# Gated differential attention: the gates between the two halves of the q, k, v projection, and a reordered prologue

## The chip, the cores and the metric

The kernel runs on one core of one Trainium2 chip. The metric is the device time of one execution in microseconds (us). Beside it stands the span, from the first to the last instruction in the profile of one execution.

## The reference

A residual layer with 1024 tokens of width 1024: row norm, a projection to q, k, v and a gate z (each 2048 wide, 16 heads), differential attention (two score maps for each head, the second subtracted with a weight lambda), a norm for each head, the product with silu(z), and the output projection.

```python
h = rms_norm(x, norm_g)
q, k, v, z = split(h @ w_in, 4)
q = rms_norm(q, q_norm_g) * 64 ** -0.5        # each head: 2 maps of width 64
k = rms_norm(k, k_norm_g)
# causal, with ALiBi bias, for each head and map m
probs = softmax(q_m @ k_m.T - slope * dist)
o = (probs[0] - lam * probs[1]) @ v           # v: 128 wide
o = rms_norm(o, head_norm_g) * (1 - lam0)
return x + (o * silu(z)) @ w_out
```

Products are made in split form: an operand is written as a high part in float16 and a low part (the remainder), and three products (high x high, low x high, high x low) are added in PSUM.

## The kernel before, in words

Everything runs on the core's five engines under a framework that places the instructions of each engine in an order by a simulated timeline; the program's order is a preference, and an instruction moves ahead where its operands are there. Calls inside `pin(...)` (`keep_in_program_order`) keep the program's order among themselves on their engine. Each engine then runs its own list in order.

*Prologue* (lines 217 to 345). For each of eight tiles of 128 tokens, `chain(t)` makes the row norm: a Square on ScalarE (L255), `rsqrt` (VectorE L94, ScalarE's Ln and Exp in L98 and L99, VectorE L100, L101, L103), and the normed tile `htok` by VectorE in L259. TensorE transposes it into PSUM (L275), ScalarE copies the high part `h` out (L277), VectorE makes the low part (L278). The gain `gb` is brought to a power-of-two unit first: its maximum (L240), the unit sg[0] (L241 to L244), and the product with the whole gain (L245). In between stands the split of the first head's weights, `split_w`, a generator that is advanced step by step: eight row maxima (L154), their maximum over the partitions by a product on TensorE (L165, L169), the scales (L172 to L180), the high part on ScalarE (L199), the low part on VectorE (L205, for q and k) or on GpSimd (L202 and L203, for v and the gate: `LO_POOL`).

*Heads.* The loop at line 669 takes the heads in the order 1, 3, ..., 15, 0, 2, ..., 14. In round i, `merge` runs two generators side by side: `attend` of the head before and `project` of this head, at a set ratio (RATE). `project` makes, for two halves c of 512 tokens, four groups of q, k, v (24 matmuls each, L370 to L372) into PSUM tiles `pg`, which ScalarE (L422, L423) and VectorE (L424) copy out, and behind each half `norm(c, rw)` (L376 to L396), which ends in a DMA transpose on SyncE's queue (L393) and two copies (L396). After both halves come the two gates, one for each half (`gate`, L443 to L459): 24 matmuls into a tile `pz` of the same three PSUM banks (`PSG` = 3, tag "pg"), and a chain of six steps over ScalarE and VectorE (L452 to L457) that makes silu; L457 is the last to read the bank. Heads 10, 12 and 14 (`LATE`) make no gate here; theirs come at the end in `late_gates`. Between the groups `prepare` advances the split of the next head's weights: four squares (L160), a step with a small product that needs a free part of a PSUM tile `pb` (and waits where `pb` is None), then L199, L202, L203, L205. In the first head `prepare` is called twice a group, in the others once, and again in the gates.

`attend` makes, for eight steps of 128 queries, the scores on TensorE (L570), a row minimum with the bias on VectorE (L559), the exponentials on ScalarE (L576), the difference and its split (L584, L66, L587) and a DMA transpose on SyncE's queue (L589); the values (L601 to L603) and the head's norm (L609 to L631) follow. Steps 0 to 3 read the first half's q and k, steps 4 to 7 the second's. `finalize` multiplies with the gate.

## Time and profile before

| | us |
|---|---|
| median of 3 runs | 1176.29 |
| lowest and highest | 1174.27, 1181.22 |
| the profiled execution | 1173.53 |
| its span | 1171.8 |
| TensorE busy (share of the span) | 1109.9 (95%) |
| VectorE busy | 883.0 (75%) |
| ScalarE busy | 774.2 (66%) |
| GpSimd busy | 272.2 (23%) |

In the rows, PE is TensorE's matmuls, PEld its weight loads, DVE VectorE, ACT ScalarE, POOL GpSimd, SP SyncE, which issues DMAs; L12 is line 12 of the kernel. A row of the timeline has the start in us, the duration in us, the engine, the line, the operation, output <- inputs, shapes and the count; in brackets stands the idle time of the engine ahead of it and who ended it. Matmuls overlap in the engine, so their durations add up to more than the time.

### The profile page before, as it was taken

The page shows a single profiled execution, that of the slowest core. Times are in us where ns is not written, and L with a number is a line of the kernel's source. Part 1 is how long each engine was busy: PE and PEld are TensorE (multiplying, and loading weights), DVE is VectorE, ACT ScalarE, POOL GpSimd, SP SyncE. Part 2 cuts the span into 40 slices and gives each one's busy share as a digit, 9 for nine tenths or more (in the row PEclk, how much of TensorE's full clock was granted, in tenths as well). Part 3 has the DMA queues.
Part 4 walks back from the last instruction along what each step waited for, and adds up shares of the span by engine and source line. Part 5 has one row for each costly group of instructions (what it writes and reads, how often), then busy time and mean ns, then how long its engine had stood idle before and what let it go on. Part 6 is the DMA issues. An engine that isn't in the chain of part 4 may idle for free.

```text
span 1171.8 us, 18439 instructions
## 1 busy us (share of the span) xinstructions
PE 1109.9 (95%) x6154; PEld 668.5 (57%) x6154; DVE 883.0 (75%) x2180; ACT 774.2 (66%) x1713; POOL 272.2 (23%) x208
## 2 busy tenths in 40 slices
PE   4999999999999999999999999999899997999998
PEld 3555554545555555555545455555455534788887
DVE  6867869787978797879787878788888898563121
ACT  4757778787878797869686978787778776230000
POOL 2220314141314131314131313312121302031000
PEclk7999999999999999999999999999999988999999
DMA  7453736464646464646463645464564457685342
GB/s 222 109 119 52 164 67 140 89 140 85 139 90 137 88 143 89 146 80 133 93 144 76 140 93 126 93 129 100 105 137 87 109 125 182 143 292 179 112 130 70
DMA packets 327887, 143.50 MB, mean 122 GB/s; under 512 B 225136, under 2 KB 307312, under 8 KB 327792
## 3 DMA queue, kind: packets, MB, share of 16 engines
q1 hardware_dynamic: 323040, 133.93, 50.9%
q10 hardware_dynamic: 4752, 8.39, 2.7%
q8 instruction: 48, 0.79, 0.3%
q14 instruction: 47, 0.39, 0.1%
HBM read 63.11 MB, written 16.25 MB: 68 GB/s over the span
## 4 chain that ended last, share of the span: by engine, by line
PE 51%; DVE 20%; ACT 10%; issue 8%; DMA 6%; POOL 2%; SPq 2%; DVEq 0%; ACTq 0%; POOLq 0%
PE pg L370 8%; PE pg L371 8%; PE pg L372 8%; DVE p L559 6%; PE pf L498 5%; PE pf L499 5%; PE pf L500 5%; PE pss L570 3%; DMA raww<-in_l_w_in_dram 3%; DVE p L584 2%; ACT p L576 2%; ACT wsp L160 2%; ACT wsp L199 2%; DMA wt<-p 2%; PE po L601 2%
## 5 line engine op out<-in xcount | busy, mean ns | idle before, releaser
L370 PE MATMUL pg<-wsp,h 128*128 128x384 f16 x1024 | 336.3, 328 | 21.0 <-DVE sz L457 11.9
L372 PE MATMUL pg<-wsp,h 128*128 128x384 f16 x1024 | 336.4, 329 | 1.1 <-DVE h L278 1.1
L371 PE MATMUL pg<-wsp,h 128*128 128x384 f16 x1024 | 336.3, 328 | 1.2 <-POOL wsp L203 1.2
L576 ACT ACTIVATE p<-p,mn 128x128 f32<-128x128 f32 (+7 forms) x256 | 196.4, 768 | 61.0 <-DVE mn L559 59.8
L559 DVE CUSTOM_DVE_ANT_0 p<-pss,toep,nsl 128x512 f32<-128x512 f32 (+3 forms) x256 | 161.2, 642 | 36.8 <-DMA wt<-p 24.6
L570 PE MATMUL pss<-qk 128*128 128x512 f16 (+3 forms) x768 | 164.6, 327 | 11.6 <-DVE mn L559 11.5
L371 PEld LDWEIGHTS <-h 128*128 128x128 f16 x1024 | 100.7, 98 | 86.7 <-issue 26.5
L372 PEld LDWEIGHTS <-h 128*128 128x128 f16 x1024 | 100.6, 98 | 68.2 <-issue 3.7
L66 ACT ACTIVATE p<-p,rc 128x128 f16<-128x128 f32 (+7 forms) x128 | 98.6, 771 | 61.8 <-DVE p L584 60.7
L370 PEld LDWEIGHTS <-h 128*128 128x128 f16 x1024 | 100.7, 98 | 66.6 <-issue 4.1
L584 DVE SCALAR_TENSOR_TENSOR p<-p,rc,p 128x128 f32<-128x128 f32 (+7 forms) x128 | 116.9, 914 | 1.5
L587 DVE SCALAR_TENSOR_TENSOR p<-p,rc,p 128x128 f16<-128x128 f32 (+7 forms) x128 | 104.7, 820 | 14.8 <-ACT p L66 14.6
L570 PEld LDWEIGHTS <-qk 128*128 128x128 f16 x768 | 71.0, 98 | 72.2 <-issue 18.6
L447 PE MATMUL pz<-h,wsp 128*128 128x512 f16 x256 | 98.3, 384 | 1.3 <-DVE sz L457 1.3
L448 PE MATMUL pz<-h,wsp 128*128 128x512 f16 x256 | 98.3, 384 | 0.0
L614 POOL TENSOR_TENSOR sql<-sqo,sqh 128x512 fp32r<-128x512 f32 x30 | 41.7, 1390 | 243.3 <-ACT sqh L612 243.3
L449 PE MATMUL pz<-h,wsp 128*128 128x512 f16 x256 | 98.1, 383 | 0.0
L537 POOL TENSOR_TENSOR sz<-sqo,sz 128x512 f32<-128x512 f32 x26 | 37.7, 1448 | 184.4 <-DVE sqo L631 150.0
L202 POOL TENSOR_SCALAR raww<-raww,scw 128x1024 f32<-128x1024 f32 (+1 forms) x31 | 42.3, 1371 | 159.1 <-ACT wsp L199 127.9
L559 DVE CUSTOM_DVE_ANT_0 p<-pss,toep,mn 128x128 f32<-128x128 f32 (+3 forms) x128 | 75.6, 601 | 0.0
L160 ACT ACTIVATE wsp<-raww 128x1024 f16<-128x1024 f32 x61 | 63.6, 1044 | 14.7 <-DMA raww<-in_l_w_in_dram 9.4
L503 DVE TENSOR_TENSOR xr<-pf,xr 128x512 f32<-128x512 f32 (+1 forms) x33 | 22.1, 671 | 63.4 <-PE pf L500 62.5
(160 smaller groups left out, 2082.9 us busy)
## 6 DMA issues: line engine op xcount, KB each, us to landing
raww<-in_l_w_in_dram SPq DMA_DIRECT2D x96, 256.0 KB, 3.8
rawo<-in_l_w_out_dram SPq DMA_DIRECT2D x32, 256.0 KB, 4.5
qk<-qk SPq DMA_DIRECT2D x64, 128.0 KB, 2.4
raww<-in_l_w_in_dram SPq DMA_DIRECT2D x40, 192.0 KB, 3.7
g_dram<-sz SPq DMA_DIRECT2D x30, 256.0 KB, 2.3
rawg<-g_dram ACTq DMA_DIRECT2D x24, 256.0 KB, 3.5
xt<-in_x_dram SPq DMA_DIRECT2D x8, 512.0 KB, 5.3
xr<-in_x_dram SPq DMA_DIRECT2D x16, 256.0 KB, 3.5
```

Source lines behind the costliest of these rows:

```text
L66: A.activation(out, in_, AF.Copy, scale=scale)
L370: T.matmul(pg, a_h, w_h, start=k == 0, stop=False)
L371: T.matmul(pg, a_h, w_l, start=False, stop=False)
L372: T.matmul(pg, a_l, w_h, start=False, stop=k == KT - 1)
L447: T.matmul(pz, wt["hi"][:, k, n], hh[c][:, k], start=k == 0, stop=False)
L448: T.matmul(pz, wt["hi"][:, k, n], hl[c][:, k], start=False, stop=False)
L449: T.matmul(pz, wt["lo"][:, k, n], hh[c][:, k], start=False, stop=k == KT - 1)
L559: V.tensor_tensor_reduce(out=pm[m][:, o:o + w], in0=pss[:, :w], in1=toep[:, u:u + w], scale=nslope, scalar=3e38 if prev[m] is None else pr ...
L570: T.matmul(pss[m][:, :w].rearrange("p (t q) -> p t q", q=P), qk[:, c, 0, i % 4, m], qk[:, b, v, :w // P, m], start=v == 1, stop=v == 2)
L576: A.activation(pm[m][:, :n], pm[m][:, :n], AF.Exp, scale=-1.0, bias=prev[m], accum_out=sx[:, 1 - m:2 - m])
L584: V.scalar_tensor_tensor(out=p0, in0=p1, scalar=rc[:, 0:1], in1=p0, op0=ALU.mult, op1=ALU.add)
L587: V.scalar_tensor_tensor(out=pl[:, n:], in0=p0, scalar=rc[:, 1:2], in1=pl[:, :n], op0=ALU.mult, op1=ALU.subtract)
```

## The change

Four things. (1) The gain is no longer brought to its unit ahead of the norm: the unit sg[0] is made inside the first `rsqrt` (`gap`) and multiplied in where h is copied out of PSUM, in ScalarE's scale and in a scalar_tensor_tensor on VectorE. (2) The eight row maxima of the first weights, which stood in a block behind the first tile's copies, are called 3, 3 and 2 at a time around them (`bounds`), and the second tile's chain is interleaved with the split. (3) The first head's v block has its high part made by GpSimd instead of ScalarE, and the first product group runs all high x high products, then low x high, then high x low. (4) `project` makes the first half with its norm, then both gates, then the second half with its norm; `prepare` is called twice for each group of the first half and once for each of the second, in every head. The tile `sz` has four buffers instead of three, and `sqo` takes a buffer of the norm's `sqk`.

```diff
--- before.py
+++ after.py
@@ -87,7 +87,7 @@
     eps_t = cp.tile([P, 1], F32, name="eps_t")
     G.memset(eps_t, EPS)
 
-    def rsqrt(sp, src, n, scale, tag, pin=lambda ins: ins, eps=EPS):
+    def rsqrt(sp, src, n, scale, tag, pin=lambda ins: ins, gap=lambda: None, eps=EPS):
 
         v = sp.tile([P, n], F32, name=f"v_{tag}", tag=f"v_{tag}")
         if isinstance(eps, float):
@@ -97,6 +97,7 @@
         y = sp.tile([P, n], F32, name=f"y_{tag}", tag=f"y_{tag}")
         pin(A.activation(y, v, AF.Ln))
         pin(A.activation(y, y, AF.Exp, scale=-0.5))
+        gap()
         pin(V.tensor_tensor(v, v, y, ALU.mult))
         pin(V.scalar_tensor_tensor(out=v, in0=v, scalar=-0.5, in1=y, op0=ALU.mult, op1=ALU.mult))
         r = sp.tile([P, n], F32, name=f"r_{tag}", tag=f"r_{tag}")
@@ -193,8 +194,16 @@
             if not first:
                 rest()
             yield
+            if first:
+                for ks in (slice(0, 4), slice(4, 8)):
+                    src, h_, l_, c_ = raw[:, ks, 2], hi[:, ks, 2], lo[:, ks, 2], sc[:, 2:3]
+                    pin(G.tensor_scalar(h_, src, c_, 1.0, ALU.mult, ALU.mult))
+                for ks in (slice(0, 4), slice(4, 8)):
+                    src, h_, l_, c_ = raw[:, ks, 2], hi[:, ks, 2], lo[:, ks, 2], sc[:, 2:3]
+                    pin(G.tensor_scalar(src, src, c_, 1.0, ALU.mult, ALU.mult))
+                    pin(G.tensor_tensor(l_, src, h_, ALU.subtract))
             for ks in (slice(0, 4), slice(4, 8)) if first else (slice(0, 8),):
-                for j, s_ in enumerate(blocks):
+                for j, s_ in enumerate(blocks[:2] if first else blocks):
                     src, h_, l_, c_ = raw[:, ks, s_], hi[:, ks, s_], lo[:, ks, s_], sc[:, j:j + 1]
                     pin(A.activation(h_, src, AF.Copy, scale=c_))
                     yield
@@ -237,15 +246,17 @@
                     T.transpose(out=tp[:, k], in_=ident, identity=ident)
 
             gt_ = x1.tile([P, 1], F32, name="gt_")
-            V.tensor_reduce(out=gt_, in_=gb, axis=AX.X, op=ALU.max, apply_absolute_value=True)
-            V.tensor_scalar(gt_, gt_, 2.0 ** -20, None, ALU.max)
-            V.tensor_scalar(gt_.bitcast(I32), gt_.bitcast(I32), 0x7F800000, None, ALU.bitwise_and)
-            V.reciprocal(sg[0], gt_)
-            V.tensor_scalar(sg[0], sg[0], 2.0 ** 9, None, ALU.mult)
-            V.tensor_scalar(gb, gb, sg[0], None, ALU.mult)
-            V.tensor_scalar(sg[1], gt_, 2.0 ** -9, None, ALU.mult)
-            V.tensor_tensor(sg[2], sg[0], sg[0], ALU.mult)
-            V.tensor_scalar(sg[2], sg[2], EPS, None, ALU.mult)
+
+            def top_gain():
+                V.tensor_scalar(gt_, gt_, 2.0 ** -20, None, ALU.max)
+                pin(V.tensor_scalar(gt_.bitcast(I32), gt_.bitcast(I32), 0x7F800000, None, ALU.bitwise_and))
+                pin(V.reciprocal(sg[0], gt_))
+                pin(V.tensor_scalar(sg[0], sg[0], 2.0 ** 9, None, ALU.mult))
+
+            def gain_units():
+                V.tensor_scalar(sg[1], gt_, 2.0 ** -9, None, ALU.mult)
+                V.tensor_tensor(sg[2], sg[0], sg[0], ALU.mult)
+                V.tensor_scalar(sg[2], sg[2], EPS, None, ALU.mult)
 
             def chain(t):
                 if t > 0 and len(xts) < NB:
@@ -253,19 +264,30 @@
                 sq = xp.tile([P, D], F32, name="sqx", tag="sqx", bufs=2)
                 ss = xp.tile([P, 1], F32, name="ssx", tag="ssx")
                 pin(A.activation(sq, xts[t], AF.Square, accum_out=ss))
-                r = rsqrt(xp, ss, 1, 1.0 / D, "x", pin)
+                if t == 0:
+                    pin(V.tensor_reduce(out=gt_, in_=gb, axis=AX.X, op=ALU.max, apply_absolute_value=True))
+                yield
+                r = rsqrt(xp, ss, 1, 1.0 / D, "x", pin, gap=top_gain if t == 0 else lambda: None)
                 ht = xp.tile([P, D], F32, name="htok", tag="htok", bufs=3)
                 for cs in (slice(0, 512), slice(512, D)) if t == 0 else (slice(0, D),):
                     pin(V.scalar_tensor_tensor(out=ht[:, cs], in0=xts[t][:, cs], scalar=r, in1=gb[:, cs],
                                                op0=ALU.mult, op1=ALU.mult))
-                return ht
+                hts.append(ht)
 
             def pin(ins):
                 return tc.keep_in_program_order(ins)
 
-            hts = [chain(0)]
+            hts = []
             w0 = split_w(raw0, range(3), wt0, heads[0], True, pin)
             wt0["pb"] = lambda: ps_s.tile([P, 512], F32, name="pb", tag="pss")
+
+            def bounds(n):
+                for _ in range(n):
+                    next(w0)
+
+            for _ in chain(0):
+                pass
+            bounds(3)
             for t in range(NB):
                 ht = hts[t]
                 c, o = t // 4, (t % 4) * P
@@ -274,17 +296,25 @@
                     for k in range(4):
                         T.transpose(out=tp[:, k], in_=ht[:, (k4 * 4 + k) * P:(k4 * 4 + k + 1) * P], identity=ident)
                     dh = hh[c][:, k4 * 4:k4 * 4 + 4, o:o + P]
-                    pin(A.activation(dh, tp, AF.Copy))
-                    last_v = pin(V.tensor_tensor(hl[c][:, k4 * 4:k4 * 4 + 4, o:o + P], tp, dh, ALU.subtract))
+                    pin(A.activation(dh, tp, AF.Copy, scale=sg[0]))
+                    last_v = pin(V.scalar_tensor_tensor(out=hl[c][:, k4 * 4:k4 * 4 + 4, o:o + P], in0=tp, scalar=sg[0],
+                                                        in1=dh, op0=ALU.mult, op1=ALU.subtract))
+                    if t == 0:
+                        bounds(3 - k4)
                 if t == 0:
-                    for _ in range(KT + 1):
-                        next(w0)
-                    hts.append(chain(1))
+                    gain_units()
+                    one = chain(1)
+                    next(one)
+                    bounds(1)
+                    bounds(5)
+                    for _ in one:
+                        pass
                     for _ in w0:
                         pass
                     load_raw(heads[0], raw0, range(3, 4))
                 while len(hts) < min(t + 3, NB):
-                    hts.append(chain(len(hts)))
+                    for _ in chain(len(hts)):
+                        pass
                 if t == 4:
                     order = ExitStack()
                     order.enter_context(tc.issue_after(last_v.ins))
@@ -364,6 +394,15 @@
             shift = 8 - (hd + 2) // 2
 
             def gemm_piece(pg, c, o, ks):
+                if hd == heads[0] and c == 0 and o == 0:
+
+                    if ks[0] == 0:
+                        return
+                    for n, (a, w) in enumerate(((hh, "hi"), (hl, "hi"), (hh, "lo"))):
+                        for k in range(KT):
+                            T.matmul(pg, a[0][:, k, :P], wt[w][:, k, :3].rearrange("p s c -> p (s c)"),
+                                     start=n == 0 and k == 0, stop=n == 2 and k == KT - 1)
+                    return
                 for k in ks:
                     a_h, a_l = hh[c][:, k, o:o + P], hl[c][:, k, o:o + P]
                     w_h, w_l = (wt[v][:, k, :3].rearrange("p s c -> p (s c)") for v in ("hi", "lo"))
@@ -411,7 +450,7 @@
                         return
                     prep.pop(0)
 
-            for c in range(2):
+            def qkv(c):
                 rw = tmp.tile([P, 2, 4, P], F32, name="rw", tag="rw", bufs=2)
                 for t in range(4):
                     pb = ps_g.tile([P, 512], F32, name="pg", tag="pg")
@@ -424,19 +463,18 @@
                             V.scalar_tensor_tensor(out=vl[:, c * 4 + t], in0=pg[:, 256:], scalar=vsc,
                                                    in1=vh[:, c * 4 + t], op0=ALU.mult, op1=ALU.subtract)
                             prepare(lambda: pb[:, 384:])
-                        elif hd == heads[0]:
+                        elif c == 0:
                             prepare(None)
                         yield 2.1
                 norm(c, rw)
-            if hd in LATE:
-                while prep:
-                    prepare(None)
-                return
-            for c in range(2):
-                for k in gate(st, wt, 3, c):
-                    if k % 2:
-                        prepare(None)
-                    yield 0.69
+            yield from qkv(0)
+            if hd not in LATE:
+                for c in range(2):
+                    for k in gate(st, wt, 3, c):
+                        if k % 2:
+                            prepare(None)
+                        yield 0.69
+            yield from qkv(1)
             while prep:
                 prepare(None)
 
@@ -448,7 +486,7 @@
                 T.matmul(pz, wt["hi"][:, k, n], hl[c][:, k], start=False, stop=False)
                 T.matmul(pz, wt["lo"][:, k, n], hh[c][:, k], start=False, stop=k == KT - 1)
                 yield k
-            e = vp.tile([P, 512], F32, name="sz", tag="sz", bufs=3)
+            e = vp.tile([P, 512], F32, name="sz", tag="sz", bufs=4)
             A.activation(e, pz, AF.Exp, scale=wt["inv"][:, 1, n:n + 1])
             V.tensor_scalar(e, e, 1e18, None, ALU.min)
             A.activation(e, e, AF.Ln, bias=1.0)
@@ -605,7 +643,7 @@
                         yield 6 * (4 - il) * P / 2400
                 os = tmp.tile([P, 512], F32, name="os", tag="os")
                 A.activation(os, po, AF.Copy, scale=st["unit"])
-                sq = tmp.tile([P, 512], F32, name="sqo", tag="sqo")
+                sq = tmp.tile([P, 1024], F32, name="sqo", tag="sqk", bufs=2)[:, :512]
                 A.activation(sq, os, AF.Square)
                 sqh = tmp.tile([P, 512], F32R, name="sqh", tag="sqh")
                 e = V if hd == heads[-1] else G
```

## Rows read from the trace of the kernel before

**Rows 1.** The page, parts 1 and 2: busy time, and the granted clock in 40 slices.

```profile
PE 1109.9 (95%) x6154; PEld 668.5 (57%) x6154; DVE 883.0 (75%) x2180; ACT 774.2 (66%) x1713; POOL 272.2 (23%) x208
PEclk7999999999999999999999999999999988999999
```

**Rows 2.** TensorE's waits, whole span: who waited for whom, us, times, longest us.

```profile
PE pg L370 <- DVE sz L457: 11.9, 8, 2.3
PE pss L570 <- DVE mn L559: 11.5, 12, 2.5
...
PE pg L370 <- DVE vl L424: 5.1, 5, 1.6
```

**Rows 3.** The timeline where the sixth head ends: two gates' chains, TensorE's wait.

```profile
362.94 0.67 ACT L452 ACTIVATE sz<-pz,inv 128x512 f32<-128x512 f32 x1
...
373.78 0.74 DVE L457 SCALAR_TENSOR_TENSOR sz<-pz,inv,sz 128x512 f32<-128x512 f32 x1
...
374.58 0.32 PE L370 MATMUL pg<-wsp,h 128*128 128x384 f16 x1 [1.78 <-DVE sz L457]
...
386.69 0.75 DVE L457 SCALAR_TENSOR_TENSOR sz<-pz,inv,sz 128x512 f32<-128x512 f32 x1
```

**Rows 4.** Stretches of the next head: length, PE, PEld, DVE, ACT, POOL busy, clock, DMA.

```profile
367.40:372.30 4.90, 4.90 (x35) 3.16 (x34) 4.80 (x11) 4.90 (x9) 0.00 (x0) 1.00 0.99 209
372.30:377.20 4.90, 3.12 (x21) 1.78 (x19) 3.37 (x9) 4.90 (x13) 2.19 (x1) 1.00 0.83 87
...
391.90:396.80 4.90, 4.90 (x31) 2.85 (x29) 2.21 (x6) 3.16 (x9) 2.55 (x2) 1.00 0.51 97
```

**Rows 5.** Stretches behind two of TensorE's holes; the granted clock stands after POOL.

```profile
93.00:97.00 4.00, 4.00 (x17) 1.90 (x15) 3.25 (x12) 3.32 (x11) 0.00 (x0) 0.57 0.00 0
...
608.60:612.00 3.40, 3.40 (x13) 1.59 (x12) 1.72 (x4) 3.40 (x14) 0.00 (x0) 0.51 0.90 193
```

**Rows 6.** The timeline of the prologue, all engines, 0 to 31 us.

```profile
6.12 1.22 DVE L240 TENSOR_REDUCE gt__167<-gb 128x1 f32<-128x1024 f32 x1 [6.12 <-DMA gb<-in_l_norm_g_dram]
...
10.30 1.42 DVE L259 SCALAR_TENSOR_TENSOR htok<-xt,r_x,gb 128x512 f32<-128x512 f32 x2
...
14.31 3.76 DVE L154 TENSOR_REDUCE b<-raww 128x3 f32<-128x384 f32 x8
...
18.71 0.34 PE L169 MATMUL pb<-br,ones 128*128 128x4 f32 x1 [5.67 <-DVE br L165]
...
30.93 0.38 ACT L422 ACTIVATE rw<-pg 128x256 f32<-128x256 f32 x1 [2.21 <-PE pg L372]
```

**Rows 7.** GpSimd's L202 up to 50 us (ns min/median/max), and the timeline beside L203.

```profile
L202 POOL TENSOR_SCALAR raww<-raww,scw x3: 1117/1119/1762, 22.3 to 38.2; 128x512 f32<-128x512 f32 x2, 128x1024 f32<-128x1024 f32 x1
...
26.83 1.15 POOL L203 TENSOR_TENSOR wsp<-raww,wsp 128x512 f16<-128x512 f32 x1
...
26.95 1.05 DVE L101 SCALAR_TENSOR_TENSOR v_x<-v_x,y_x 128x1 f32<-128x1 f32 x1
...
28.03 0.16 DVE L103 SCALAR_TENSOR_TENSOR r_x<-v_x,y_x 128x1 f32<-128x1 f32 x1
```

**Rows 8.** The timeline of TensorE at the eighth tile's transposes.

```profile
59.31 0.45 PE L275 MATMUL tp<-ident,htok 128*128 128x128 f32 x1 [2.13 <-DVE htok L259]
```

**Rows 9.** The timeline of the first gate's chain in the first head.

```profile
74.82 0.67 ACT L452 ACTIVATE sz<-pz,inv 128x512 f32<-128x512 f32 x1
...
80.04 0.74 DVE L457 SCALAR_TENSOR_TENSOR sz<-pz,inv,sz 128x512 f32<-128x512 f32 x1
```

**Rows 10.** The timeline behind head 10, which makes no gate: first scores, transpose, fifth step.

```profile
830.25 0.27 PE L570 MATMUL pss<-qk 128*128 128x128 f16 x2 [1.81 <-DVE mn L559]
...
840.91 1.90 SPq L393 DMA_TRANSPOSE qk<-sqk  x1
...
855.36 1.25 PE L570 MATMUL pss<-qk 128*128 128x512 f16 x8
```

**Rows 11.** Line 393, whole span: from issue to landing.

```profile
DMA to landing us min/median/max: 4.3/4.5/6.4
```

## The prediction

> **What bounds the kernel now.** I read the page first: TensorE is busy 1109.9 of 1171.8 us and its clock is granted in full almost everywhere [rows 1]. So it is the bound, and as the change adds and removes no matmul, it can only win TensorE's idle time (61.9 us) and the stretches at half clock. The second view is TensorE's own waits: who ended them, and how much each is worth in all [rows 2]. Two stand at places that the change moves. "pg L370 <- DVE sz L457", 11.9 us in 8 waits, is a product group of a new head that finds no PSUM bank, because the gates of the head before hold them and line 457 is a gate's last reader. "pg L370 <- DVE vl L424", 5.1 us in 5 waits, is a group a little later that waits for the copies of an earlier group. The third view is the timeline of one such place [rows 3]. The first gate's chain begins with L452 at 362.94 and ends with L457 at 374.52: 11.6 us for six steps of 0.4 to 0.75 us, which queue in order behind softmax work. TensorE has other work for 9.9 of these (until 372.80) and stands the remaining 1.78. The second gate's L457 starts only at 386.69, so for 12 us more the groups turn on two banks of three, and that is where the wait on L424 comes from. The fourth view says why just there: in that head's stretches of 4.9 us [rows 4], VectorE and ScalarE are both full (4.80 and 4.90) where one head ends and the next begins, and the next stretch has TensorE's large hole (3.12 of 4.90 busy); a third of the head later both have room (2.21 and 3.16 of 4.90).
>
> Some of these holes also cost the clock. After the ones at 92 and 607 the granted clock is 0.57 in 93 to 97 and 0.51 in 608.6 to 612 [rows 5]: 4 us at 0.57 and 3.4 us at 0.51 are 1.7 us of work lost each; I say 2 us each with the edges.
>
> The program's beginning is another matter: until TensorE's first product group is complete at 30.9, a chain of small VectorE operations sets the time, which I take from the timeline step by step [rows 6].
>
> **The change, part by part.**
>
> 1. *Unit of h in the copy.* Before, the gain's maximum (L240, 6.12 to 7.34), five small operations and a product over the whole gain stand ahead of the first row norm and its L259 at 10.30 [rows 6]. After, the product is gone, and four of the small operations lie between ScalarE's Ln and Exp and the norm's last three. At 0.2 us a step (L103, 0.16, begins 0.03 after its forerunner ends [rows 7]) that is one, four and three steps: 7.34 + 1.6 = 8.9, so L259 starts 1.4 us earlier. The copies out of PSUM take a scale: L278 becomes the form of L457 with the same 512 columns out of PSUM, 0.74 [rows 3]; all but the first two lie beside TensorE's products.
>
> 2. *Row maxima as tiles land.* Eight reductions, 3.76 us in one block from 14.31 [rows 6], go 3 + 3 + 2 around the two copies of the first tile. From 8.9, VectorE's two L259 (1.42), eight reductions (3.76) and two copies (1.5) end near 15.6 instead of 18.07. Line 169 (18.71) and the scales behind it come 2.6 us earlier.
>
> 3. *The v block's high half on GpSimd, the first group in another order.* GpSimd gets two casts ahead of its four operations. The trace has no such cast; the nearest rows have the same 512 columns, 1.12 to 1.76 us [rows 7]. Six of them from 17.3 (the scales) end between 24.0 and 27.9, where the fourth ended at 27.98 before; I take 25.5, since the low prices stand where VectorE is quiet. The new order lets 16 of the first group's 24 products run without GpSimd's low half, so the group, complete at 30.9 (L422 follows at 30.93 [rows 6]), should be complete near 27: 4 us earlier, between 2.8 and 5.4. What TensorE bounds behind it moves along. Later in the first head TensorE waits 2.13 us for a row norm at 59.31 [rows 8]; the gates now offer it other work there, and I count 1 us. Together 5 us, from 9 won to 3 lost.
> Against it speaks what GpSimd does to VectorE: L101, one column wide as L103 with its 0.16, took 1.05 while GpSimd's L203 ran [rows 7]. The Trainium skill, "SBUF — State Buffer", section "Who interferes with whom", says that a VectorE instruction with two SBUF inputs and a GpSimd instruction that reads SBUF need the same port pair, an exclusive lock, so the second waits for the first. By that rule the added casts can hold up the second tile's chain, and part of the 4 us goes back; the row agrees with it.
>
> 4. *Gates between the halves.* The waits on L457 at the head's end go: the last gate now has four product groups and the attention beside them behind it before the next head begins. Gain 11.9 us [rows 2]. Of the waits on L424 I take half (2.5 us), as the squares of the next weights still stand there, and of the two half-clock stretches one (2 us) [rows 5].
> The price is the same wait in mid-head: the second group after the gates needs a gate's bank. The cover is a gate and a group, 9.9 us in [rows 3]; the chain was 11.6 us there, but 6.0 us in the first head, where no attention runs (74.82 to 80.78 [rows 9]). In mid-head VectorE has room [rows 4], so I put the chain near 9, below the cover, and charge a stray 0.3 us in each of 13 heads, 4 us. The bounds are 0 and the old wait of 1.5 us in each, 20 us.
>
> 5. *The second half's norm comes last.* Its transposes land after the next head's attention has begun. The heads without gates have that order already: attention begins at 830.25, the transpose is issued at 840.91, and the fifth score step, its first reader, runs at 855.36 [rows 10]. TensorE has products of the next head to run meanwhile; on SyncE the softmax's transposes queue behind this one. I charge 1 us. Bounds: nothing, and 2.5 us in each of 13 heads (the longest wait of scores on a row minimum, "mn L559" [rows 2]), 32 us.
>
> 6. *The next weights split sooner.* The extra step in the first half brings the squares and the split, which lie beside TensorE, forward. In the first head the step that needs a bank is held until after the gates and has only three groups to hide it instead of three and two gates; with everything 4 us earlier I count nothing, up to 3 us if it shows. A fourth sz buffer and the shared buffer of sqo cost nothing while no three users of its two live at once.
>
> **The sum.** 5 + 11.9 + 2.5 + 2 - 4 - 1 = 16.4 us. The profiled execution took 1173.5 us, so it would take 1157. It lies 2.8 us under the median of the three runs, 1176.3; against that median I say 1160 us.
>
> **Rivals.**
> - *All of it goes.* No wait in mid-head, no half clock, 9 us at the beginning: 9 + 11.9 + 5.1 + 4 = 30, so 1146 us. For it: VectorE's room in mid-head [rows 4]. Against: norm and squares stay at the boundary.
> - *The wait only moves.* The gate's chain is as long in mid-head, since the norm of the first half and the split of the next weights are queued with it; the 5 us of the beginning remain: 1171 us.
> - *The second half comes too late (slower).* Each head's fifth score step waits for the transposes. It decides when they land later than the products queued ahead of that step last. 32 us less the 17 won: 1191 us. Against it: in the head of [rows 10] 14.4 us lie between issue and use, and a transpose lands 4.5 us after its issue [rows 11].
> - *The beginning gains nothing.* GpSimd's six operations hold VectorE's small steps for 1 us each as in [rows 7], the first group is no earlier or 3 us later, the rest is as forecast: 1168 us with the 3 us. This is what the page's rule would do.
>
> **How the numbers follow.** Forecast 0.48, all goes 0.14, wait moves 0.20, too late 0.10, nothing at the beginning 0.08. The forecast's own spread is 1154 to 1167. To hold 8 in 10 the range goes from 1147, the edge of "all goes", to 1178, past the moved wait and its bounds. A measurement of this kernel tells about 0.5%, 5.9 us, from no change: faster is below 1170.4, slower above 1182.2. Forecast and "all goes" are faster (0.62), of the moved wait under half (0.08), of the last rival most (0.05): 0.75. Slower: most of "too late" and a trace of the moved wait, 0.10. The same: the remaining 0.15.
>
> **What would show it.** Right: TensorE's waits on L457 fall below 4 us in all, and none stands at a head's first scores; no half clock near the first attention; the reductions end near 15.6 and the first group near 27. Wrong: 10 us or more on L457 in mid-head; score steps that wait for transposed q and k; GpSimd's first casts over 1.8 us with small VectorE steps of 1 us beside them; first scores no earlier than before.

## The result and the profile after

The changed kernel took 1184.96 us (median of 7 runs, 1182.62 to 1187.03) where the kernel before took 1175.21 beside it (7 runs): a ratio of 1.0081, 95% interval 1.0062 to 1.0099. It is slower by 0.8%, where 1160 us was forecast. The profiled execution took 1182.71 us, with a span of 1180.8.

The page of the kernel after, parts 1 and 2, against [rows 1]:

```profile
PE 1110.6 (94%) x6154; PEld 668.4 (57%) x6154; DVE 900.0 (76%) x2179; ACT 769.8 (65%) x1711; POOL 279.0 (24%) x210
PEclk7989899999999999999999999999999989999999
```

TensorE's busy time is unchanged, so its idle time rose from 61.9 to 70.2 us, and that is nearly the whole difference of the spans (1180.8 against 1171.8). TensorE's waits over the span of the kernel after, against [rows 2]; columns as there:

```profile
PE po L639 <- DMA wt<-p: 15.4, 8, 3.0
PE tp L297 <- DVE htok L273: 14.4, 3, 11.1
PE pss L608 <- DVE mn L597: 11.3, 15, 1.9
PE pg L403 <- ACT wsp L208: 5.6, 2, 3.9
...
PE pz L485 <- DVE sz L495: 3.9, 1, 3.9
PE pss L608 <- DMA qk<-qk: 3.0, 3, 2.1
...
PE pg L409 <- DVE sz L495: 0.5, 3, 0.2
```

The bank waits that the change aimed at are gone: there the gate's last reader (L495, L457 before) costs the product groups 0.5 us instead of 11.9, and the copies of vl (L424 before, 5.1) appear no more. The same reader still costs 3.9 us in one wait of the late gates (`pz` L485, at 961.54; 1.3 before), so 4.4 us are left in all. Two new ones stand in their place. "po L639 <- DMA wt<-p" is the values of the attention that wait for the transposed softmax: 15.4 us in 8 waits, 10.7 of them between 235 and 800 us. "tp L297 <- DVE htok L273" is the eighth tile's transposes: one wait of 11.1 us. Around the latter the timeline of the kernel after reads:

```profile
54.30 1.06 ACT L161 ACTIVATE wsp<-raww 128x1024 f16<-128x1024 f32 x1 [2.14 <-DMA raww<-in_l_w_in_dram]
...
57.11 0.14 DVE L94 TENSOR_SCALAR v_x<-ssx 128x1 f32<-128x1 f32 x1
...
58.38 0.19 ACT L161 ACTIVATION_READ_ACCUMULATOR wsp<-raww 128x1 f32 x1
...
59.94 0.19 ACT L98 ACTIVATE y_x<-v_x 128x1 f32<-128x1 f32 x1
...
61.92 1.28 DVE L273 SCALAR_TENSOR_TENSOR htok<-xt,r_x,gb 128x1024 f32<-128x1024 f32 x1
...
63.35 1.94 PE L297 MATMUL tp<-ident,htok 128*128 128x128 f32 x8 [11.10 <-DVE htok L273]
...
65.20 0.40 PE L608 MATMUL pss<-qk 128*128 128x128 f16 x2
```

The eighth tile's L94 runs on VectorE only at 57.11; its Ln (L98) then stands on ScalarE behind the last square of the next weights (L161), which came late by DMA, a square of the first half's norm and a step of a gate; and its L273 behind that. The second gate needs h of all eight tiles, and ahead of the second half's groups it is next in TensorE's order, so TensorE has nothing else to do: the transposes come 4 us later than before (63.35 against 59.31 [rows 8]), and the wait grows from 2.13 to 11.1 us. The stretches of the kernel after at this hole and at two later places (columns as in [rows 4]):

```profile
58.00:63.00 5.00, 0.00 (x0) 0.00 (x0) 3.52 (x7) 4.07 (x9) 0.00 (x0) 0.50 0.19 37
63.00:67.00 4.00, 3.65 (x15) 2.52 (x16) 3.69 (x6) 1.37 (x2) 0.00 (x0) 0.50 0.63 121
...
130.00:134.00 4.00, 0.43 (x2) 0.10 (x1) 3.17 (x9) 3.95 (x8) 0.00 (x0) 0.81 1.01 208
134.00:138.00 4.00, 3.94 (x15) 2.13 (x16) 4.00 (x8) 2.52 (x5) 0.00 (x0) 0.50 1.06 296
182.00:190.00 8.00, 5.77 (x34) 3.14 (x33) 8.00 (x15) 5.01 (x10) 3.44 (x2) 1.00 0.43 121
190.00:196.00 6.00, 2.10 (x6) 0.67 (x6) 6.00 (x16) 3.54 (x9) 0.00 (x0) 0.83 1.03 206
```

Read TensorE's busy time first: nothing at 58, 0.43 of 4 us at 130, 2.10 of 6 at 190. Behind the first two holes the clock is granted at half (0.50, the 1.2 GHz level). At 182 to 196 VectorE is full (14.00 of 14 us). These are three neighbouring heads: the first, the second and the third.

**Where the time goes.** To find the loss I set each matmul's start against the time that the matmuls ahead of it would take at full clock (for each shape the lower quartile of its spacing in the kernel before). The difference is how late TensorE is, in us, after so much work, in one profiled execution of each kernel; h, p, q and n are experiments below.

| work done, us | before | after | h_late_new | p_late1 | q_late3 | n_undo_early |
|---|---|---|---|---|---|---|
| 40 | 27.2 | 34.9 | 29.0 | 28.3 | 28.7 | 30.5 |
| 80 | 31.1 | 36.2 | 31.9 | 32.4 | 31.5 | 35.4 |
| 100 | 31.1 | 44.4 | 31.8 | 41.1 | 31.4 | 35.3 |
| 160 | 31.3 | 52.6 | 39.1 | 48.3 | 31.6 | 43.7 |
| 200 | 34.4 | 52.7 | 39.2 | 48.4 | 36.5 | 43.8 |
| 750 | 55.9 | 76.3 | 64.6 | 71.3 | 58.5 | 67.1 |
| end | 85.6 | 94.7 | 84.0 | 90.6 | 79.8 | 86.6 |

After is 18.3 us behind before by 200 us of work, three heads or so. From there to 750 it loses 23.6 and before 21.5: the middle heads gain nothing. At the end it loses 18.4 and before 29.7.

### The profile page after: what moved, and what is told of

Same layout as the page of the kernel before. It is cut to its first block, busy times and chain, and to the rows that moved or that the text cites. A ratio compares the mean times of both kernels' runs of the same rounds, so it can differ in the third digit from the quotient of the medians.

```text
span 1180.8 us, 18379 instructions
## 1 busy us (share of the span) xinstructions
PE 1110.6 (94%) x6154; PEld 668.4 (57%) x6154; DVE 900.0 (76%) x2179; ACT 769.8 (65%) x1711; POOL 279.0 (24%) x210
## 4 chain that ended last, share of the span: by engine, by line
PE 68%; DVE 13%; DMA 7%; issue 5%; ACT 4%; SPq 2%; POOL 1%; DVEq 0%; ACTq 0%; POOLq 0%
PE pg L409 11%; PE pg L411 11%; PE pg L410 10%; PE pss L608 6%; PE pf L536 5%; PE pf L537 5%; PE pf L538 5%; DMA wt<-p 4%; DVE p L597 4%; PE pz L485 3%; PE pz L487 3%; PE pz L486 3%; PE po L639 2%; PE po L640 2%; PE po L641 2%
## 5 line engine op out<-in xcount | busy, mean ns | idle before, releaser
L410 PE MATMUL pg<-wsp,h 128*128 128x384 f16 x1016 | 332.9, 328 | 0.7 <-POOL wsp L212 0.7
L409 PE MATMUL pg<-wsp,h 128*128 128x384 f16 x1016 | 332.9, 328 | 0.6 <-DVE sz L495 0.5
L411 PE MATMUL pg<-wsp,h 128*128 128x384 f16 x1016 | 332.5, 327 | 0.0
L614 ACT ACTIVATE p<-p,mn 128x128 f32<-128x128 f32 (+7 forms) x256 | 196.0, 768 | 57.9 <-DVE mn L597 44.4
L608 PE MATMUL pss<-qk 128*128 128x512 f16 (+3 forms) x768 | 167.5, 328 | 14.5 <-DVE mn L597 11.3
L66 ACT ACTIVATE p<-p,rc 128x128 f16<-128x128 f32 (+7 forms) x128 | 98.1, 770 | 39.2 <-DVE p L622 32.1
L625 DVE SCALAR_TENSOR_TENSOR p<-p,rc,p 128x128 f16<-128x128 f32 (+7 forms) x128 | 108.4, 848 | 9.3 <-ACT p L66 9.3
L622 DVE SCALAR_TENSOR_TENSOR p<-p,rc,p 128x128 f32<-128x128 f32 (+7 forms) x128 | 109.9, 866 | 1.1
L485 PE MATMUL pz<-h,wsp 128*128 128x512 f16 x256 | 98.0, 383 | 3.9 <-DVE sz L495 3.9
L211 POOL TENSOR_SCALAR raww<-raww,scw 128x1024 f32<-128x1024 f32 x29 | 46.0, 1598 | 167.3 <-ACT wsp L208 117.3
L575 POOL TENSOR_TENSOR sz<-sqo,sz 128x512 f32<-128x512 f32 x26 | 44.3, 1703 | 166.6 <-DVE sqo L669 114.4
L639 PE MATMUL po<-wt,vh 128*128 128x512 f16 x192 | 63.4, 330 | 19.2 <-DMA wt<-p 15.4
L208 ACT ACTIVATE wsp<-raww,scw 128x1024 f16<-128x1024 f32 (+1 forms) x65 | 67.8, 1111 | 3.6 <-DVE scw L181 3.5
```

The lines of the kernel that those rows point to most:

```text
L66: A.activation(out, in_, AF.Copy, scale=scale)
L409: T.matmul(pg, a_h, w_h, start=k == 0, stop=False)
L410: T.matmul(pg, a_h, w_l, start=False, stop=False)
L411: T.matmul(pg, a_l, w_h, start=False, stop=k == KT - 1)
L485: T.matmul(pz, wt["hi"][:, k, n], hh[c][:, k], start=k == 0, stop=False)
L608: T.matmul(pss[m][:, :w].rearrange("p (t q) -> p t q", q=P), qk[:, c, 0, i % 4, m], qk[:, b, v, :w // P, m], start=v == 1, stop=v == 2)
```

## The experiments

Each comes as what differs from the kernel named; ratios are to the kernel before on the same chip, with the 95% interval. "New order" is first half, gates, second half, with the added calls of `prepare`.

**One half of the change at a time.** a_prologue is the changed kernel with the old `project`, b_project has the old prologue with the new `project`.

```diff
# a_prologue, against after (buffers as before)
-            yield from qkv(0)
-            if hd not in LATE: ... both gates ...
-            yield from qkv(1)
+            for c in range(2): ... both halves, then both gates ...
# b_project, against before
-            for c in range(2): ... both halves, then both gates ...
+            yield from qkv(0)
+            if hd not in LATE: ... both gates ...
+            yield from qkv(1)
```

> The prologue of the change alone; the order of the projection, of prepare and the buffers as before. Theory 1 (the loss is made in the first head, where TensorE stands 11.1 us for the eighth tile's transposes because of the order gates - second half): no loss here, 1172 to 1176 us, since the first group is only 1.7 us earlier and that is taken back by the fifth tile. Theory 2 (the loss is made in every head by the crowd in mid-head): 1170 us, the prologue's gain stays whole.

> The new order of projection, prepare and buffers alone, with the prologue as before. Theory 1: TensorE has the same hole of about 11 us ahead of the eighth tile's transposes; 1184 to 1187 us. Theory 2: the waits of the values on the softmax's transposes cost 15 us in all and the prologue's gain is missing; 1188 to 1192 us.

a_prologue: 1175.56 us, 1.0023 (1.0005 to 1.0042). b_project: 1181.89 us, 1.0087 (1.0057 to 1.0117). The loss is the new order's, and the prologue gives nothing by itself.

**First theory: the hole at the eighth tile is the loss.** c_firsthead gives the first head alone its old order back.

```diff
# c_firsthead, against after
+            if hd == heads[0]:
+                yield from qkv(1)
...
-            yield from qkv(1)
+            if hd != heads[0]:
+                yield from qkv(1)
```

> The change, but the first head keeps the old order (both halves, then both gates) and its two steps of prepare for each group. Theory 1: the hole of 11.1 us goes and the whole loss with it; 1173 to 1176 us, a wait of about 2 us left at the eighth tile. Theory 2: the later heads take most of it back, since VectorE bounds them; 1181 to 1185 us.

1184.29 us, 1.0086 (1.0054 to 1.0117). The wait of 11.1 us is gone and the time is the same, so this theory falls. TensorE's timeline in the second head shows what came instead:

```profile
135.17 0.48 PE L409 MATMUL pg<-wsp,h 128*128 128x384 f16 x1 [7.80 <-DVE sz L498]
```

This is the price that the forecast put on mid-head, a group without a bank, in one piece of 7.8 us. In the kernel after the same head's gate chain is nearly as long: its six steps, L490 to L495, run from 120.02 for the first gate until 133.97. There the profile names other waits for the hole at 130, two of scores on row minima (1.17 and 1.51 us) and one of scores on the copies of transposed q and k (2.07 us); the bank comes free at about the same time, so without them the group would have waited until 133.97 as well:

```profile
120.02 0.67 ACT L490 ACTIVATE sz<-pz,inv 128x512 f32<-128x512 f32 x1
...
124.76 0.82 DVE L491 TENSOR_SCALAR sz<-sz 128x512 f32<-128x512 f32 x1
...
133.22 0.75 DVE L495 SCALAR_TENSOR_TENSOR sz<-pz,inv,sz 128x512 f32<-128x512 f32 x1
...
134.06 0.82 PE L608 MATMUL pss<-qk 128*128 128x128 f16 x4 [2.07 <-DMA qk<-qk]
```

**Second theory: each head's values wait.** d_values6 places the values one score step later, so that the softmax's transposes have landed.

```diff
# d_values6, against after
-VALUES_AT = 5
-NORM_AT = 6
+VALUES_AT = 6
+NORM_AT = 7
```

> The change with the first values a score step later (after step 6) and the head's norm after step 7, so that the transposes that the values wait for have landed. Theory 1: the 15.4 us of waits on these transposes go but are other work's waits in truth; 1181 to 1185 us, the hole at the eighth tile stays. Theory 2: these waits are the loss; 1170 to 1174 us.

1198.12 us, 1.0230 (1.0195 to 1.0265). TensorE's waits there:

```profile
PE pss L608 <- DVE mn L597: 28.3, 20, 2.5
...
PE po L639 <- DMA wt<-p: 7.9, 4, 2.0
```

The values' wait halves, and the scores' wait on the row minima goes from 11.3 to 28.3 us. The wait moved and grew. I read it so that the heads between are held by the softmax and not by where one reader of it stands; as a cure the theory falls.

**Third theory: the first heads, not all heads.** Old prologue; h_late_new has the new order only from the third head on, i_early_new only in the first two.

```diff
# h_late_new, against b_project
-            if hd not in LATE: ... gates between the halves ...
+            new = place[hd] >= 2
+            if new and hd not in LATE: ... gates between the halves ...
# i_early_new, against h_late_new
-            new = place[hd] >= 2
+            new = place[hd] < 2
```

> Prologue of before; the first two heads keep the old order of projection and prepare, the other heads take the new one (with its buffers). Theory 3 (start-up: the new order costs some 20 us in the first two heads, where the eighth tile and the second half's q and k come late, and gives some 10 us back in the last heads): 1162 to 1170 us, faster than before, less what the change of order between the second and the third head costs. Theory 2 (each head costs): 1180 us or more.

> Prologue of before; the first two heads take the new order, all others the old one. Theory 3: the loss of the start without the gain of the end, 1185 to 1195 us. Theory 2: two heads of sixteen, 1174 to 1177 us.

h_late_new: 1172.0 us, 0.9975 (0.9961 to 0.9989). i_early_new: 1189.03 us, 1.0119 (1.0096 to 1.0142). The new order is worth a little from the third head on. With the first two heads alone changed the kernel is 14 us slower; by the lateness of the table above 10.9 us of it are there after 100 us of work (42.0 against 31.1). TensorE's waits in h_late_new:

```profile
PE po L606 <- DMA wt<-p: 17.8, 11, 2.2
PE pss L575 <- DVE mn L564: 8.7, 13, 1.9
```

So even here the values wait 17.8 us, about as much as the bank waits that went (11.9 and 5.1).

**One head at a time.**

```diff
# against h_late_new
-            new = place[hd] >= 2
+            new = place[hd] == 0      # l_head0
+            new = place[hd] == 1      # m_head1
+            new = place[hd] >= 10     # j_last
+            new = place[hd] >= 16     # k_lateprep: no head; LATE heads call prepare once more a group
```

> Prologue of before; only the first head takes the new order. Theory 3a (the hole ahead of the eighth tile and the late first attention stay as loss): 1180 to 1185 us. Rival (later heads make it up): 1173 to 1177 us.

> Prologue of before; only the second head takes the new order, where the gates' chains meet the whole first attention. Theory 3b (the chains of some 18 us hold two of three PSUM banks, and TensorE stands some 8 us): 1180 to 1184 us. Rival (only the first head's delay made that wait): 1173 to 1176 us.

> Prologue of before; only the heads from the eleventh on (six of sixteen, the last three without gates) take the new order and the earlier prepare. Theory 4 (the last heads really gain some 12 us by the new order): 1163 to 1169 us. Rival (the last heads only give back what was lost before, since VectorE bounds them and TensorE's delay no longer counts there): 1172 to 1177 us.

> Prologue and order of before; the earlier prepare in the three heads without gates alone, with the new buffers. Theory 4a (the gain of the last heads is the earlier split of the next weights): 1164 to 1169 us. Theory 4b (it is the order of the gates in the heads before): 1172 to 1176 us.

l_head0: 1182.29 us, 1.0061 (1.0045 to 1.0077). m_head1: 1187.22 us, 1.0105 (1.0089 to 1.0122). j_last: 1177.51 us, 1.0020 (0.9999 to 1.0040). k_lateprep: 1174.45 us, 0.9996 (0.9984 to 1.0008). Each of the first two heads loses alone; the last six places gain nothing measurable alone. The buffers and the added `prepare` of the last heads cost nothing together, but the trace of k_lateprep shows two parts that cancel. Up to its last three heads it differs from the kernel before in the buffers alone. There, between 160 and 750 us of work, it loses 29.1 us where before loses 24.6, and behind 750 it loses 23.5 where before loses 29.7. TensorE's waits on the gates' banks from 235 to 800 us, in k_lateprep and before:

```profile
PE pg L370 <- DVE sz L463: 17.5, 9, 2.8
```

```profile
PE pg L370 <- DVE sz L457: 10.3, 6, 2.3
```

l_head0, m_head1, i_early_new and o_head0_split (below) have 17.5 to 17.6 us on these banks in that stretch too, and a_prologue, with the old buffers, has 10.7. So the new buffers make the heads that keep the old order lose some 4 us, and the times of the runs with few new heads hold that cost as well; which of the two buffers does it is open. The two holes, from the timelines of l_head0 and of m_head1:

```profile
62.08 1.94 PE L275 MATMUL tp<-ident,htok 128*128 128x128 f32 x8 [7.97 <-DVE htok L259]
```

```profile
130.31 0.48 PE L370 MATMUL pg<-wsp,h 128*128 128x384 f16 x1 [7.30 <-DVE sz L463]
```

**The gates apart.** Both have first half, first gate, second half, second gate in every head; g_split_oldpro has the old prologue.

```diff
# f_split, against after
-                for c in range(2): ... gate c ...
+                yield from gated(0)
             yield from qkv(1)
+            if hd not in LATE:
+                yield from gated(1)
```

> The change, but with the second half's gate behind the second half's groups: first half, its gate, second half, its gate. Theory 3: nothing in the first head needs the eighth tile before the second half's groups, so the hole of 11 us goes, and the second half's norm begins one gate (5 us) earlier; half or more of the loss goes, 1172 to 1179 us. Theory 2: the gates still crowd the heads, 1181 to 1186 us.

> The same split order of the gates with the prologue of before. Theory 3: 1 to 3 us less than with the new prologue (which alone cost 2.4 us), 1169 to 1177 us. Theory 2: 1180 to 1184 us.

f_split: 1216.41 us, 1.0349 (1.0316 to 1.0382). g_split_oldpro: 1218.88 us, 1.0373 (1.0355 to 1.0391). Far worse than expected, and with either prologue. f_split is ahead of before after 80 us of work (26.2 us late against 31.1) and loses 68.0 us between 200 and 750, so the loss lies in the heads between. Their waits (values on the softmax's transposes 21.5 and 23.4 us, longest 4.5) say where TensorE stands, not why a parted pair of gates does this; that stays open.

**The rest of the cause.** After these, it was open whether the changed kernel itself is cured by undoing two heads, what the first head's share is made of, and whether the second and the third lose when all heads behind them are new.

```diff
# n_undo_early, against after: h_late_new's project
+            new = place[hd] >= 2
# o_head0_split, against l_head0: first half, first gate, second half, second gate in the first head
-            if new and hd not in LATE: ... both gates ...
+            if new: ... first gate ...
# against h_late_new
-            new = place[hd] >= 2
+            new = place[hd] >= 1      # p_late1
+            new = place[hd] >= 3      # q_late3
+            new = place[hd] >= 6      # r_late6
```

> The changed kernel with its prologue and its buffers, in which the first two heads alone go back to the order of the kernel before (both halves, then both gates); all other heads keep the gates between the halves. If the loss is made in the first two heads, this undoes it: the old prologue with the same later heads gave a ratio of 0.9975, the new prologue alone cost 0.23%, so 0.998 to 1.001 and a time near 1174 us, some 10 us under the changed kernel. If instead the new prologue and the new order harm each other, it stays above 1.005 (1180 us or more).

> Old prologue, old order in all heads but the first, whose parts go: first half, first gate, second half, second gate. The first gate needs four row tiles, the second gate all eight, and here four product groups stand ahead of it. If what the new order costs in the first head (1.0061 with the first head alone changed) comes of the second gate's need of all eight tiles, TensorE's wait for the eighth row norm (7.97 us there) falls to about 2 and the ratio to within 0.25% of 1.000. If it comes of the order of the heads behind it, or of the norm of the second half coming last, the ratio stays near 1.005.

> Old prologue; the gates between the halves in all heads but the first. If the second head is a place of loss of its own, this stands 0.5% to 1% above the version that begins with the third head (0.9975): ratio 1.003 to 1.008, with TensorE waiting 5 us or more near 130 us on the last reader of a gate (line 462) or on q and k of the second half. If only the first head matters when the others are all changed, it stays near 0.998.

> Old prologue; the gates between the halves from the fourth head on. If the third head is as good a place as the later ones, the time is that of the version that begins with the third head, ratio 0.996 to 0.999. If the third head loses as well (in the changed kernel TensorE stands 5.6 us between 185 and 196 us), this is faster still, 0.993 to 0.995.

> Old prologue; the gates between the halves only from the seventh head on (place 6). With the start at the fourth head the ratio was 0.9936, with the eleventh 1.002. If the gain comes head by head in the middle of the program, seven of the ten heads give 0.995 to 0.998. If it comes only where the last heads are reached, whatever the middle does, it stays at 0.993 to 0.995.

- n_undo_early: 1173.48 us, 0.9994 (0.9977 to 1.0011). Undoing the new order in two heads takes the whole loss back, and prologue and order don't harm each other.
- o_head0_split: 1175.23 us, 0.9998 (0.9982 to 1.0015), against 1.0061 with both gates in front. The first head's share comes of the second gate standing ahead of the second half: with it go the wait for all eight tiles (7.97 us in l_head0) and a wait of 1.80 us on the second half's transposed q and k.
- p_late1: 1180.05 us, 1.0046 (1.0030 to 1.0062). The second head loses by itself.
- q_late3: 1167.65 us, 0.9936 (0.9914 to 0.9957), faster than both kernels and than h_late_new: the third head loses as well. h_late_new's stretch that q_late3 lacks, then q_late3 and the kernel before in the same stretch:

```profile
172.00:182.00 10.00, 5.09 (x26) 2.57 (x26) 10.00 (x21) 5.86 (x12) 2.19 (x1) 0.92 0.83 189
```

```profile
172.00:182.00 10.00, 10.00 (x61) 5.59 (x59) 9.62 (x29) 9.84 (x18) 5.41 (x4) 1.00 0.41 82
```

```profile
172.00:182.00 10.00, 10.00 (x59) 5.44 (x57) 9.60 (x28) 9.94 (x16) 5.76 (x4) 1.00 0.38 74
```

- r_late6: 1173.64 us, 0.9997 (0.9979 to 1.0015). Neither expectation: the gain of q_late3 is gone when the new order starts three heads later, so it is neither the end's alone nor so much for each head. By lateness the two differ by 0.7 us after 750 us of work (59.2 against 58.5) and by 4.8 at the end (84.5 against 79.7), where both have the same order. Why the last heads then give back less stays open.

The wait behind p_late1's loss, from TensorE's timeline:

```profile
131.36 0.48 PE L370 MATMUL pg<-wsp,h 128*128 128x384 f16 x1 [6.54 <-DVE sz L462]
```

## Why the prediction was wrong, step by step

The step that failed is the fourth, and with it what the third and the sixth said of the first head. Of the 16.4 us, 14.4 were waits on banks booked as time won; these waits went, other waits came, and the first three heads lost 18.3 us.

**1. Unit of h in the copy: right.** L273 begins at 8.69 (forecast 8.9).

```profile
8.69 1.42 DVE L273 SCALAR_TENSOR_TENSOR htok<-xt,r_x,gb 128x512 f32<-128x512 f32 x2
...
14.14 1.01 DVE L155 TENSOR_REDUCE b<-raww 128x3 f32<-128x384 f32 x2
...
17.05 1.36 POOL L200 TENSOR_SCALAR wsp<-raww,scw 128x512 f16<-128x512 f32 x2 [15.54 <-DMA raww<-in_l_w_in_dram]
17.61 1.06 ACT L161 ACTIVATE wsp<-raww 128x1024 f16<-128x1024 f32 x1 [3.56 <-DMA raww<-in_l_w_in_dram]
...
18.38 0.69 POOL L203 TENSOR_SCALAR raww<-raww,scw 128x512 f32<-128x512 f32 x1
...
18.67 1.93 ACT L208 ACTIVATE wsp<-raww,scw 128x512 f16<-128x512 f32 x3
19.41 2.55 DVE L214 SCALAR_TENSOR_TENSOR wsp<-raww,scw,wsp 128x512 f16<-128x512 f32 x2 [0.25 <-ACT wsp L208]
...
20.04 1.46 PE L403 MATMUL pg<-wsp,h 128*128 128x384 f16 x4 [3.91 <-ACT wsp L208]
20.29 1.13 POOL L203 TENSOR_SCALAR raww<-raww,scw 128x512 f32<-128x512 f32 x1
21.50 1.46 POOL L204 TENSOR_TENSOR wsp<-raww,wsp 128x512 f16<-128x512 f32 x1
...
22.40 0.71 ACT L208 ACTIVATE wsp<-raww,scw 128x512 f16<-128x512 f32 x1
...
23.16 4.48 PE L403 MATMUL pg<-wsp,h 128*128 128x384 f16 x16 [1.66 <-ACT wsp L208]
...
28.35 0.81 PE L403 MATMUL pg<-wsp,h 128*128 128x384 f16 x4
...
30.31 0.38 ACT L461 ACTIVATE rw<-pg 128x256 f32<-128x256 f32 x1
```

**2. Row maxima: right.** In these rows of the prologue after (as [rows 6]) the reductions end at 15.15 (forecast 15.6), and the scales are there for GpSimd at 17.05.

**3. The first group: size and carry were wrong.** GpSimd was not what ended last. Its two casts took 0.69 us each (two in 1.36, overlapping a little), below the bound of 1.12 to 1.76, and its six steps ended at 22.96 (forecast 25.5). But ScalarE's casts (L208) began only at 18.67, behind the square of the gate's block (L161), which waited for its DMA, and the fourth only at 22.40, behind the second tile's small steps, which stood behind L214. TensorE waited 3.9 and 1.7 us for L208 (5.6 in all). The first group is complete at 29.16 (forecast 27, before 30.9), 1.7 us earlier where 4 were forecast, and its copy, L461, starts at 30.31 instead of 30.93. I had costed the engine that got the added work, not the queue on which the rest of the cast still stood. The term of 5 us was worth nothing: alone the prologue measures +0.2%. In a_prologue a later group waits 3.9 us for the low part of h (L300, at 56.95), 1.1 before (L278), which takes back more than the 1.7.

The rule of the Trainium skill that I set against this step ("SBUF — State Buffer", section "Who interferes with whom": one shared port pair, an exclusive lock) is borne out here. In a stretch of four heads the norm's step v_k of 16 columns (L101 before, L102 after) went from 170 to 447 ns, which is what the two lines below say, before and after (their last columns: busy us, mean ns):

```profile
L101 DVE SCALAR_TENSOR_TENSOR v_k<-v_k,y_k 128x16 f32<-128x16 f32 x8 | 1.4, 170 | 0.1
```

```profile
L102 DVE SCALAR_TENSOR_TENSOR v_k<-v_k,y_k 128x16 f32<-128x16 f32 x8 | 3.6, 447 | 0.0
```

Two of the eight steps make the difference; the other six took 165 to 172 ns. Each of the two fell under GpSimd's product with the gate (L575) and ended with it, here at 307.76 and 307.73:

```profile
306.03 1.70 POOL L575 TENSOR_TENSOR sz<-sqo,sz 128x512 f32<-128x512 f32 x1 [2.74 <-DVE v_k L101]
306.48 1.28 DVE L102 SCALAR_TENSOR_TENSOR v_k<-v_k,y_k 128x16 f32<-128x16 f32 x1
```

VectorE's busy time rose from 883.0 to 900.0 us, 8.1 of it in the split of the weights, before and after:

```profile
L205 DVE SCALAR_TENSOR_TENSOR wsp<-raww,scw,wsp 128x1024 f16<-128x1024 f32 x32 | 40.1, 1285 | 1.9 <-ACT wsp L199 1.9
```

```profile
L214 DVE SCALAR_TENSOR_TENSOR wsp<-raww,scw,wsp 128x1024 f16<-128x1024 f32 x32 | 48.2, 1519 | 5.9 <-ACT wsp L208 5.9
```

This alone doesn't decide: in h_late_new and q_late3, both faster than before, VectorE is busy 895.3 and 891.0 us, and the step v_k has 444 and 303 ns. How much it adds to the loss of after no run shows.

**4. Gates between the halves: the 11.9 us went as forecast, and the time did not.** The groups' waits on L457's line fell to 0.5 us (4.4 with the late gate's, a little over the 4 set as a sign), and those on L424 are gone. What failed is that I booked a wait that goes as time won. In the heads between, TensorE's idle time came back as values that wait for transposed softmax (15.4 us over the span), and when those were placed later (d_values6), as scores that wait for row minima. My reading is that the softmax's chain sets the pace there; it is argued, not shown by a run of its own. o_head0_split ends at the time of before although it is 4 us ahead of it by the first head's end (26.7 us late against 31.1 after 70 us of work), but it is no witness for this: it waits 20.3 us on the gates' banks instead of 11.9, and so does k_lateprep (20.5), which has no such lead; that is the buffers. Of the rivals, "the wait only moves" had this mechanism, with another place: 15.4 us on the values and not on a bank.

The charge for mid-head was wrong in kind. I put the chain near 9 us in each of 13 heads and gave each the same stray 0.3 us. It cost nothing in most heads and 6.5 to 7.8 us in one, the second (c_firsthead, m_head1, p_late1), where the whole chain meets the first attention on VectorE. [rows 9], from a head with no attention beside it, could not show that, and [rows 4] are of a head further on, with the gates elsewhere.

The 2 us for the clock went the other way: half clock stands behind the holes at 58 and 130 in place of those of [rows 5].

**5. The second half's norm last: as a wait, near its charge.** The heads of [rows 10] have TensorE work between; the first attention has little. Its fifth score step runs at 106.82 after, when the q and k issued at 102.33 have landed, and at 89.58 before. In all heads together the direct wait on transposed q and k is 3.0 us, against 1 charged, but 2.07 of it are the second head's first scores, which need its first half (134.06). The longest wait on the second half's is 1.80 us, in l_head0 (at 109.39). That the first attention is late costs no more by itself: l_head0 is 36.2 us late after 80 us of work and 36.4 after 160. So the rival "too late", whose 1191 us lie nearest to the result, is near by chance: it had 32 us on this wait.

**6. Next weights sooner: the first head is where it showed.** I counted nothing, up to 3 us. The squares stand ahead of the eighth tile's norm on ScalarE, and with the gates in front TensorE waits for that tile: 11.1 us in after, 7.97 in l_head0, none of it left with one gate in front (o_head0_split). In step 3 I had counted 1 us won because the gates offer TensorE other work at that tile; the second gate needs that very tile. Alone, the first head costs 5.2 us of lateness (l_head0), the 1.80 us of step 5 among them.

**What this adds up to.** The mean over heads hid the start. By lateness, alone changed, the first head costs 5.2 us (l_head0 at 100 us of work: 36.3 against 31.1), the second 9.6 (m_head1, 40.7); the third costs 4.8 with all heads behind it new (h_late_new at 200). After is 18.3 behind there. The three don't simply add: the first two together cost 10.9 (i_early_new), and c_firsthead, which undoes the first alone, gains nothing, since its second head loses 9.6 us (35.0 to 44.6 from 80 to 100 us of work) where that of after loses 8.2. Undoing the first two together took the whole loss back (n_undo_early). Part of the loss comes back at the program's end, by the table: after loses 11 us less than before from 750 us of work on. Not separated: the place of the gates and the added calls of `prepare`, which every run of the new order has together.

## What to carry to other kernels

Price a reordering of a loop at its first rounds apart from its steady rounds: what a moved step needs (here all eight tiles, or a quiet VectorE) may not be there yet, and a few blocked steps at the head of an in-order queue can cost as much as many small waits save (18 us against 17 here). A wait that disappears is time won only if the engine that sets the pace of that stretch has room; look at the next chain's busy time before booking it. Such an order can be switched on by round: from the fourth head on it made this kernel 0.6% faster, from the seventh on it made no difference, so the round to begin with has to be measured. Two changes that come together can hide each other: the new buffers cost the old order some 4 us, and only a trace by stage showed it.

## What the runs showed of the hardware

GpSimd's cast of 128x512 from f32 to f16 with a scale took 0.69 us where VectorE was quiet, and so did its scaling of 128x512 in place (L203 at 18.38); beside VectorE's L214 the same scaling took 1.13 us (at 20.29). Where the two meet, either can be the one that waits: VectorE's step v_k of 16 columns took 1.28 us under GpSimd's L575 instead of 0.17, and ended 0.03 us after it.
